# Transformer layer in split float32 on one core: products of the middle pieces alternate between the two token tiles

## The chip, the core and the metric

The kernel runs on one of the eight cores of a Trainium2 chip. The metric is the device time of one execution in microseconds. Three runs of the kernel before took 646.57, 647.06 and 647.47 us; the median is 647.06 us.

## What is computed

One layer of a hybrid network on 256 tokens of width 1024, in float32: a gated feed-forward block, a mixing block whose two arms are a causal depthwise convolution and an attention of 16 heads, and a second feed-forward block. Cut to the matrix products, which are nearly all of the work:

```python
x = x + 0.5 * swiglu(rms_norm(x, ffn1_norm), ffn1_w_gate, ffn1_w_up, ffn1_w_down)   # 1024 -> 2 x 2816 -> 1024
proj = rms_norm(x, mix_norm) @ w_in                                               # 1024 -> 7 x 1024
conv_a, conv_b, q, k, v, gate_a, gate_b = jnp.split(proj, SPLITS, axis=-1)
y_a = silu(layer_norm(causal_depthwise_conv(conv_a * sigmoid(conv_b), ...))) @ w_conv_proj
y_b = attention(q, k, v) @ w_attn_proj                     # 16 heads of 64, causal over 256 tokens
x = x + (sigmoid(gate_a) * y_a + sigmoid(gate_b) * y_b) @ w_out
x = x + 0.5 * swiglu(rms_norm(x, ffn2_norm), ffn2_w_gate, ffn2_w_up, ffn2_w_down)
```

## The kernel before, in words

**Tiles.** The 256 tokens are two token tiles of 128 rows, t = 0 and 1. A chunk is 512 output columns of a weight matrix (`CH`); it needs two accumulators of 128 x 512 float32, one for each token tile, and each fills one PSUM bank. The tag `acc` has three such tiles (line 67), so two chunks in a row share one bank between them. `tr`, three tiles, takes transposes and the attention's small products.

**Split float32.** Every operand is kept as two tiles of type float32r, a rounded `hi` and a rest `lo`; a product is three matmuls, hi by hi, hi by lo and lo by hi. The stationary operand is the transposed activation (`ah(k, t)` and `al(k, t)`, 128 x 128), the moving one is the weight piece (`wh`, `wl`, 128 x 512).

**`gemm` (lines 137 to 178).** A chunk is worked off in pieces of two k-tiles (`KP`): four pieces where the depth is 1024, eleven where it is 2816. For each piece SyncE's queue loads `raw` (line 151), ScalarE rounds it to `hi` (line 100, a cast), and VectorE or GpSimd subtracts to make `lo` (line 102). There are five buffers each of `raw`, `hi` and `lo` (line 37), so the cast of a piece waits until TensorE has read the `hi` of the piece five before it. Then come twelve matmuls (lines 159 to 167): for t, for the two k-tiles, the three products. The first chunk of all runs through `gemm_first` (line 106), which the change leaves alone.

**Other TensorE work.** Between pieces TensorE gets what other parts left in `later` and `bg`: transposes (lines 211, 359, 385, 438, 509, 649) and, in the input projection, the attention, which is a generator advanced by `side`: scores (line 463, four matmuls for a pair of heads, in the upper and the lower 64 rows), `flip` and values (line 524, four matmuls). ScalarE and VectorE do the softmax, the convolution's taps and the norms.

**Who orders it.** The program is recorded in this order, but `schedule_with_timeline_sim=True` (line 824) lets a scheduler of the compiler order each engine's instructions anew by its own estimate of their times; the order on every engine is fixed when the program is built. So a change in `gemm` can move instructions anywhere.

**The seam the prediction speaks of.** `conv_act` (lines 378 to 400) stands between the attention projection and the convolution projection: sixteen transposes of `ynat` into four `tr` tiles (line 385), then on ScalarE a load of the activation table, two Silu activations for each tile (`z`, line 392) and a cast to `u2h` (line 398), then `u2l` on VectorE (line 399). `u2h` and `u2l` are the stationary operands of the next projection.

Of the kernel before, what the change touches and what calls it, by code (L numbers as in the profile page):

```python
# [50 lines left out]
class Build:  # L51
# [85 lines left out]
    def gemm(self, w, c, n, kt, ah, al, pump=0, pool=0.0, split_k=None, side=None):  # L137


        nc = self.nc  # L140
        acc = [self.acc(), self.acc()]
        k0 = 0
        npiece = 0
        sizes = list(split_k) if split_k else []
        while sum(sizes) < kt:
            sizes.append(min(KP, kt - sum(sizes)))
        for kp in sizes:
            raw = self.wp.tile([P, KP * CH], F32, tag="raw", name="raw", bufs=RAW_BUFS)
            hi = self.wp.tile([P, KP * CH], F32R, tag="hi", name="hi", bufs=HI_BUFS)
            lo = self.wp.tile([P, KP * CH], F32R, tag="lo", name="lo", bufs=LO_BUFS)  # L150
            self.last_dma = nc.sync.dma_start(
                raw[:, : kp * n].rearrange("p (k n) -> p k n", n=n), w(c, k0, kp)
            )
            self.share += pool
            pool_lo = self.share >= 1.0
            if pool_lo:
                self.share -= 1.0
            self.split(raw[:, : kp * n], hi[:, : kp * n], lo[:, : kp * n], pool_lo)
            for t in range(2):
                o = acc[t][:, :n]  # L160
                for j in range(kp):
                    k = k0 + j
                    wh, wl = hi[:, j * n : (j + 1) * n], lo[:, j * n : (j + 1) * n]
                    st, sp = k == 0, k == kt - 1
                    nc.tensor.matmul(o, ah(k, t), wh, start=st, stop=False)  # L165
                    nc.tensor.matmul(o, ah(k, t), wl, start=False, stop=False)  # L166
                    nc.tensor.matmul(o, al(k, t), wh, start=False, stop=sp)  # L167
            k0 += kp
            npiece += 1
            if npiece == LATER:  # L170
                self.flush()
            if side is not None:
                self.side += side[1]
                while self.side >= 1:
                    self.side -= 1
                    next(side[0], None)
            self.pump(pump)
        return acc
# [656 lines left out]
```

## Time and profile before

| what | us |
|---|---|
| median of three runs | 647.06 |
| the profiled execution's own time | 646.76 |
| its span, first to last instruction | 644.9 |
| TensorE matmul busy | 638.5 |
| VectorE busy | 371.6 |
| ScalarE busy | 365.9 |
| GpSimd busy | 163.1 |
| DMA, share of 16 engines | 55.5% |

The span is 1.86 us shorter than the execution's own time, which in turn lies 0.30 us under the median. Matmuls overlap in the profile: the duration of one is given as 0.39 us, while the next starts 0.23 us after it, so the busy time of TensorE says only that it is hardly ever empty; its pace is read from the starts.

### The profile page before, as it was taken

What the parts mean: (1) busy time and instruction counts of PE and PEld (TensorE: products, weight loads), DVE (VectorE), ACT (ScalarE), POOL (GpSimd) and SP (SyncE); (2) the same over time, 40 slices, a digit from 0 to 9 for tenths busy, and PEclk for the clock granted to TensorE, in tenths of its full rate; (3) what the DMA queues carried; (4) which work ended last, traced back from release to release, by engine and by line L of the source; (5) the groups of instructions that cost most, each with busy time, mean ns of one, the idle gap of its engine ahead of it and who ended that gap; (6) DMA issues with size and microseconds to landing.
All of it is one profiled execution on the core that took longest, in us unless ns stands there. A gap on an engine that the chain in (4) does not pass through costs nothing.

```text
span 644.9 us, 8142 instructions
## 1 busy us (share of the span) xinstructions
PE 638.5 (99%) x2952; PEld 517.1 (80%) x2952; DVE 371.6 (58%) x625; ACT 365.9 (57%) x549; POOL 163.1 (25%) x83
## 2 busy tenths in 40 slices
PE   9999999999999999999999999999999999999997
PEld 7788888888888888777777778788888888888886
DVE  5655464564552699879314835685664546365541
ACT  6755354443545676977987676944655435444330
POOL 0100000000006999599757564000100000000000
PEclk9999999999999999999999999999999999999999
DMA  8966655567564555544544444364755656556730
GB/s 278 353 228 194 197 170 195 161 194 224 170 200 136 182 167 185 172 131 145 177 153 147 148 146 132 131 223 135 228 161 186 197 175 201 188 167 195 202 124 33
DMA packets 32855, 114.97 MB, mean 178 GB/s; under 512 B 3632, under 2 KB 4912, under 8 KB 32816
## 3 DMA queue, kind: packets, MB, share of 16 engines
q1 hardware_dynamic: 32816, 114.46, 55.5%
q8 instruction: 23, 0.38, 0.2%
q14 instruction: 16, 0.13, 0.1%
HBM read 113.40 MB, written 1.05 MB: 177 GB/s over the span
## 4 chain that ended last, share of the span: by engine, by line
PE 67%; ACT 0%; DVE 0%; issue 0%; DVEq 0%
PE acc L165 20%; PE acc L166 20%; PE acc L167 20%; PE tr L463 2%; PE tr L524 1%; PE tr L211 1%; PE tr L509 1%; PE tr L438 1%; PE tr L359 0%; PE tr L649 0%; ACT z L392 0%; PE tr L385 0%; ACT u2h L398 0%; DVE un L640 0%; DVE ot L748 0%
## 5 line engine op out<-in xcount | busy, mean ns | idle before, releaser
L100 ACT CAST hi<-raw 128x1024 fp32r<-128x1024 f32 (+1 forms) x216 | 223.4, 1037 | 221.2 <-PE acc L167 187.6
L102 DVE TENSOR_TENSOR lo<-raw,hi 128x1024 fp32r<-128x1024 f32 (+1 forms) x156 | 186.6, 1199 | 169.7 <-ACT hi L100 165.3
L102 POOL TENSOR_TENSOR lo<-raw,hi 128x1024 fp32r<-128x1024 f32 x60 | 142.9, 2404 | 213.2 <-ACT hi L100 213.2
L347 DVE SCALAR_TENSOR_TENSOR cv<-uT,cst,cv 128x255 f32<-128x255 f32 (+28 forms) x240 | 95.4, 469 | 10.6 <-ACT cv L343 10.4
L166 PE MATMUL acc<-lo,h1h 128*128 128x512 f32 x224 | 89.0, 397 | 0.0
L165 PE MATMUL acc<-hi,h1h 128*128 128x512 f32 x224 | 88.3, 399 | 0.2 <-DVE un L640 0.2
L167 PE MATMUL acc<-hi,h1l 128*128 128x512 f32 x224 | 87.0, 394 | 0.0
L165 PE MATMUL acc<-hi,h2h 128*128 128x512 f32 x176 | 69.1, 393 | 0.0
L165 PE MATMUL acc<-hi,aTh 128*128 128x512 f32 x176 | 68.8, 391 | 0.0
L167 PE MATMUL acc<-hi,aTl 128*128 128x512 f32 x176 | 68.5, 389 | 0.0
L166 PE MATMUL acc<-lo,aTh 128*128 128x512 f32 x176 | 68.5, 389 | 0.0
L166 PE MATMUL acc<-lo,h2h 128*128 128x512 f32 x176 | 68.5, 390 | 0.0
L167 PE MATMUL acc<-hi,h2l 128*128 128x512 f32 x176 | 67.2, 390 | 0.0
L166 PE MATMUL acc<-lo,hTh 128*128 128x512 f32 x160 | 62.4, 390 | 0.5 <-DVE lo L102 0.5
L165 PE MATMUL acc<-hi,hTh 128*128 128x512 f32 x160 | 62.2, 392 | 0.0
L167 PE MATMUL acc<-hi,hTl 128*128 128x512 f32 x160 | 62.1, 389 | 0.0
L165 PEld LDWEIGHTS acc<-hi,h1h 128*128 128x128 f32 x224 | 42.1, 188 | 11.2 <-issue 2.0
L166 PEld LDWEIGHTS acc<-lo,h1h 128*128 128x128 f32 x224 | 42.1, 188 | 9.4 <-issue 1.7
L167 PEld LDWEIGHTS acc<-hi,h1l 128*128 128x128 f32 x224 | 42.1, 188 | 9.1 <-issue 0.8
L167 PEld LDWEIGHTS acc<-hi,aTl 128*128 128x128 f32 x176 | 33.0, 188 | 6.9
L165 PEld LDWEIGHTS acc<-hi,h2h 128*128 128x128 f32 x176 | 33.0, 188 | 6.8
L165 PEld LDWEIGHTS acc<-hi,aTh 128*128 128x128 f32 x176 | 33.0, 188 | 6.8
(138 smaller groups left out, 788.7 us busy)
## 6 DMA issues: line engine op xcount, KB each, us to landing
raw<-w_in SPq DMA_DIRECT2D x56, 512.0 KB, 4.3
raw<-w2gu SPq DMA_DIRECT2D x44, 512.0 KB, 4.5
raw<-w1gu SPq DMA_DIRECT2D x40, 512.0 KB, 4.7
raw<-w1d SPq DMA_DIRECT2D x22, 512.0 KB, 4.4
raw<-w2d SPq DMA_DIRECT2D x22, 512.0 KB, 4.5
raw<-w_attn SPq DMA_DIRECT2D x8, 512.0 KB, 3.9
raw<-w_conv SPq DMA_DIRECT2D x8, 512.0 KB, 4.0
raw<-w_out SPq DMA_DIRECT2D x8, 512.0 KB, 4.2
```

The costliest lines, as they stand in the source:

```text
L100: nc.scalar.copy(hi, raw)
L102: ins = eng.tensor_tensor(lo, raw, hi.bitcast(F32), ALU.subtract)
L165: nc.tensor.matmul(o, ah(k, t), wh, start=st, stop=False)
L166: nc.tensor.matmul(o, ah(k, t), wl, start=False, stop=False)
L167: nc.tensor.matmul(o, al(k, t), wh, start=False, stop=sp)
L211: nc.tensor.transpose(ps[:, q * S + t * P : q * S + (t + 1) * P], src(t, j + q), self.ident)
L347: nc.vector.scalar_tensor_tensor(o, u, w, o, ALU.mult, ALU.add)
L438: nc.tensor.transpose(ps[:, q * S + t * P : q * S + (t + 1) * P], xs[t][:, (j + q) * P : (j + q + 1) * P], self.ident,)
L463: nc.tensor.matmul(ps[q][:, t * P : t * P + (t + 1) * P], qT[r, b * S + t * P : b * S + (t + 1) * P], kT[r, b * S : b * S + (t + 1) * P], ...
L509: nc.tensor.transpose(ps[:, i * P : (i + 1) * P], pr[:, o : o + P], self.ident)
L524: nc.tensor.matmul(ps[q * HD : (q + 1) * HD, kt * P : S], v[:, kt * D + h * HD : kt * D + (h + 1) * HD], pT[:, o : o + n], start=kt == 0, ...
```

## The change

In every piece but the first and the last of a chunk the loop over the token tiles goes inside: for each k-tile hi by hi goes to t = 0 and then to t = 1, then lo by hi to both, then hi by lo to both. In the first and the last piece the outer loop over t stays. Everywhere the order of the three products of one k-tile becomes hi by hi, activation's lo by weight's hi, activation's hi by weight's lo; before, the weight's lo came second. The number of matmuls, their operands and sizes, the loads and the casts stay as they are.

```diff
-            for t in range(2):
-                o = acc[t][:, :n]
+            ts = ((0,), (1,)) if k0 == 0 or k0 + kp == kt else ((0, 1),)
+            for tt in ts:
                 for j in range(kp):
                     k = k0 + j
                     wh, wl = hi[:, j * n : (j + 1) * n], lo[:, j * n : (j + 1) * n]
                     st, sp = k == 0, k == kt - 1
-                    nc.tensor.matmul(o, ah(k, t), wh, start=st, stop=False)
-                    nc.tensor.matmul(o, ah(k, t), wl, start=False, stop=False)
-                    nc.tensor.matmul(o, al(k, t), wh, start=False, stop=sp)
+                    for a, w_part, i in ((ah, wh, 0), (al, wh, 1), (ah, wl, 2)):
+                        for t in tt:
+                            nc.tensor.matmul(
+                                acc[t][:, :n], a(k, t), w_part, start=st and i == 0,
+                                stop=sp and i == 2,
+                            )
```

In the built programs all three products now stand on line 167, and every later line is numbered three higher (385 becomes 388, 392 becomes 395, 463 becomes 466, 524 becomes 527). `gemm` works off 208 pieces in all; 118 of them are neither first nor last, and in 44 of them all twelve products alternate as built, since the scheduler orders the rest in other ways. Of the neighbouring products of 512 columns with nothing between, 362 pairs changed bank before and 799 do now; 790 pairs had the same stationary tile before and none has now.

**TensorE, second chunk, its first piece (hi_231, lo_232), before.** `acc_228` is t = 0, `acc_229` t = 1; hTh and hTl are the activation's two parts.

```order
L165 MATMUL acc_228<-hi_231,hTh_72 128x512
L165 MATMUL acc_229<-hi_231,hTh_72 128x512
L166 MATMUL acc_228<-lo_232,hTh_72 128x512
L167 MATMUL acc_228<-hi_231,hTl_73 128x512
L165 MATMUL acc_228<-hi_231,hTh_72 128x512
```


The same place now:

```order
L167 MATMUL acc_228<-hi_231,hTh_72 128x512
L167 MATMUL acc_228<-hi_231,hTl_73 128x512
L167 MATMUL acc_229<-hi_231,hTh_72 128x512
L167 MATMUL acc_229<-hi_231,hTl_73 128x512
L167 MATMUL acc_228<-lo_232,hTh_72 128x512
```


Four products that need only `hi` stand ahead of the first that needs `lo`; before there were two.

**TensorE, its second piece (hi_249, lo_250), before.**

```order
L165 MATMUL acc_228<-hi_249,hTh_72 128x512
L165 MATMUL acc_229<-hi_249,hTh_72 128x512
L166 MATMUL acc_228<-lo_250,hTh_72 128x512
L167 MATMUL acc_228<-hi_249,hTl_73 128x512
L165 MATMUL acc_228<-hi_249,hTh_72 128x512
L166 MATMUL acc_228<-lo_250,hTh_72 128x512
L167 MATMUL acc_228<-hi_249,hTl_73 128x512
L166 MATMUL acc_229<-lo_250,hTh_72 128x512
```


The same place now:

```order
L167 MATMUL acc_228<-hi_249,hTh_72 128x512
L167 MATMUL acc_229<-hi_249,hTh_72 128x512
L167 MATMUL acc_228<-hi_249,hTl_73 128x512
L167 MATMUL acc_229<-hi_249,hTl_73 128x512
L167 MATMUL acc_228<-lo_250,hTh_72 128x512
L167 MATMUL acc_229<-lo_250,hTh_72 128x512
L167 MATMUL acc_228<-hi_249,hTh_72 128x512
L167 MATMUL acc_229<-hi_249,hTh_72 128x512
```


Before, four of the twelve steps from the piece's first product to the first of the next piece change the accumulator; now all twelve do.

**TensorE, input projection, values of one pair of heads (`tr_2714`) and the score of another (`tr_2745`, `tr_2746`), before.**

```order
L524 MATMUL tr_2714<-pT_2621,v_1542 64x256 x2
L524 MATMUL tr_2714<-pT_2621,v_1542 64x128 x2
L166 MATMUL acc_2803<-lo_2849,h1h_104 128x512
L167 MATMUL acc_2803<-hi_2848,h1l_105 128x512
L165 MATMUL acc_2803<-hi_2848,h1h_104 128x512
L166 MATMUL acc_2803<-lo_2849,h1h_104 128x512
L167 MATMUL acc_2803<-hi_2848,h1l_105 128x512
L165 MATMUL acc_2802<-hi_2890,h1h_104 128x512
L166 MATMUL acc_2802<-lo_2891,h1h_104 128x512
L167 MATMUL acc_2802<-hi_2890,h1l_105 128x512
L463 MATMUL tr_2745<-kT_1541,qT_1540 128x128
L463 MATMUL tr_2746<-kT_1541,qT_1540 128x128
L463 MATMUL tr_2745<-kT_1541,qT_1540 128x256
L463 MATMUL tr_2746<-kT_1541,qT_1540 128x256
```


The same place now:

```order
L527 MATMUL tr_2714<-pT_2621,v_1542 64x256 x2
L527 MATMUL tr_2714<-pT_2621,v_1542 64x128 x2
L466 MATMUL tr_2745<-kT_1541,qT_1540 128x128
L466 MATMUL tr_2745<-kT_1541,qT_1540 128x256
L167 MATMUL acc_2802<-hi_2848,h1l_105 128x512
L167 MATMUL acc_2803<-hi_2848,h1l_105 128x512
L167 MATMUL acc_2802<-lo_2849,h1h_104 128x512
L167 MATMUL acc_2803<-lo_2849,h1h_104 128x512
L466 MATMUL tr_2746<-kT_1541,qT_1540 128x128
L466 MATMUL tr_2746<-kT_1541,qT_1540 128x256
```


The score was one run of four; now its upper half (`tr_2745`) directly follows the values and its lower half (`tr_2746`) comes four products later.

**TensorE and ScalarE at the seam.** First TensorE before: the last piece of the attention projection is hi_3642, `u2h` belongs to the convolution projection.

```order
L165 MATMUL acc_3586<-hi_3642,oh_1543 128x512
L166 MATMUL acc_3586<-lo_3643,oh_1543 128x512
L167 MATMUL acc_3586<-hi_3642,ol_1544 128x512
L165 MATMUL acc_3586<-hi_3642,oh_1543 128x512
L385 MATMUL tr_3541<-ident_91,ynat_1539 128x128 x3
L385 MATMUL tr_3551<-ident_91,ynat_1539 128x128 x3
L385 MATMUL tr_3561<-ident_91,ynat_1539 128x128 x3
L166 MATMUL acc_3586<-lo_3643,oh_1543 128x512
L167 MATMUL acc_3586<-hi_3642,ol_1544 128x512
L385 MATMUL tr_3571<-ident_91,ynat_1539 128x128 x4
L165 MATMUL acc_3663<-hi_3666,u2h_3459 128x512
```


Now:

```order
L167 MATMUL acc_3586<-hi_3642,oh_1543 128x512
L167 MATMUL acc_3586<-hi_3642,ol_1544 128x512
L167 MATMUL acc_3586<-lo_3643,oh_1543 128x512
L388 MATMUL tr_3541<-ident_91,ynat_1539 128x128 x3
L388 MATMUL tr_3551<-ident_91,ynat_1539 128x128 x3
L388 MATMUL tr_3561<-ident_91,ynat_1539 128x128 x3
L388 MATMUL tr_3571<-ident_91,ynat_1539 128x128 x4
L167 MATMUL acc_3663<-hi_3666,u2h_3459 128x512
```


ScalarE before (line 100 casts a piece, line 392 is Silu with its table load, line 398 makes `u2h`):

```order
L100 CAST hi_3702<-raw_3701 128x1024
L100 CAST hi_3720<-raw_3719 128x1024
L392 ACT_TABLE_LOAD
L392 ACTIVATE z_3546<-tr_3541,cst_70 128x256 x2
L392 ACTIVATE z_3556<-tr_3551,cst_70 128x256 x2
L398 CAST u2h_3459<-z_3546 128x512
L100 CAST hi_3744<-raw_3743 128x1024
L398 CAST u2h_3459<-z_3556 128x512
```


Now:

```order
L100 CAST hi_3702<-raw_3701 128x1024
L100 CAST hi_3720<-raw_3719 128x1024
L100 CAST hi_3744<-raw_3743 128x1024
L395 ACT_TABLE_LOAD
L395 ACTIVATE z_3546<-tr_3541,cst_70 128x256 x2
L395 ACTIVATE z_3556<-tr_3551,cst_70 128x256 x2
L401 CAST u2h_3459<-z_3546 128x512
L401 CAST u2h_3459<-z_3556 128x512
```


On TensorE the two products between the transposes of the last run went ahead of them, and the run is now thirteen transposes with nothing between. On ScalarE the cast of hi_3744 moved from behind the first `u2h` to ahead of the table load. hi_3744 is the fifth cast after hi_3642 and takes its buffer.

The start of a chunk in the input projection (before: line 165 into `acc_1657`, then line 165 into `acc_1658`, which waits) differs in one row: now a second product into `acc_1657`, activation's lo by the same hi, stands between the two.

## Rows read from the trace of the kernel before

**Rows 1.** The page: span, busy time of the engines, TensorE's clock in 40 slices.

```profile
span 644.9 us, 8142 instructions
...
PE 638.5 (99%) x2952; PEld 517.1 (80%) x2952; DVE 371.6 (58%) x625; ACT 365.9 (57%) x549; POOL 163.1 (25%) x83
...
PEclk9999999999999999999999999999999999999999
```

**Rows 2.** TensorE waits from 30 us on: engine, line, releaser: total us, times, longest.

```profile
PE acc L165 <- ACT u2h L398: 0.8, 1, 0.8
PE acc L165 <- DVE un L640: 0.2, 1, 0.2
```

**Rows 3.** Timeline of TensorE, one bank (start us, duration us, engine, line, operation, count).

```profile
28.23 0.39 PE L165 MATMUL acc<-hi,hTh 128*128 128x512 f32 x1
...
30.95 0.39 PE L165 MATMUL acc<-hi,hTh 128*128 128x512 f32 x1
```

**Rows 4.** Timeline of TensorE, second piece of the second chunk, four bank changes.

```profile
20.07 0.62 PE L165 MATMUL acc<-hi,hTh 128*128 128x512 f32 x2
20.52 0.39 PE L166 MATMUL acc<-lo,hTh 128*128 128x512 f32 x1
...
22.79 0.39 PE L165 MATMUL acc<-hi,hTh 128*128 128x512 f32 x1
```

**Rows 5.** Timeline, second chunk begins (TensorE; bracket: idle before and releaser).

```profile
16.58 0.63 PE L165 MATMUL acc<-hi,hTh 128*128 128x512 f32 x2
...
17.69 0.51 PE L166 MATMUL acc<-lo,hTh 128*128 128x512 f32 x1 [0.47 <-DVE lo L102]
```

**Rows 6.** Timeline of TensorE at the start of a chunk of the input projection.

```profile
207.75 0.39 PE L165 MATMUL acc<-hi,h1h 128*128 128x512 f32 x1
...
208.30 0.50 PE L165 MATMUL acc<-hi,h1h 128*128 128x512 f32 x1 [0.16 <-DVE un L640]
```

**Rows 7.** Timeline of TensorE: split scores, then whole values and a whole score, each with what follows.

```profile
276.47 0.86 PE L524 MATMUL tr<-pT,v 128*64 128x256 f32 x6
277.26 0.92 PE L463 MATMUL tr<-kT,qT 64*128 64x128 f32 x4
278.11 0.50 PE L166 MATMUL acc<-lo,h1h 128*128 128x512 f32 x1
...
279.69 0.92 PE L463 MATMUL tr<-kT,qT 64*128 64x128 f32 x4
280.54 0.50 PE L166 MATMUL acc<-lo,h1h 128*128 128x512 f32 x1
...
314.74 0.87 PE L524 MATMUL tr<-pT,v 128*64 128x256 f32 x8
315.54 0.50 PE L166 MATMUL acc<-lo,h1h 128*128 128x512 f32 x1
...
317.61 0.93 PE L463 MATMUL tr<-kT,qT 64*128 64x128 f32 x8
318.46 0.50 PE L165 MATMUL acc<-hi,h1h 128*128 128x512 f32 x1
```

**Rows 8.** Timeline of TensorE and ScalarE between the attention and the convolution projection.

```profile
402.88 0.39 PE L167 MATMUL acc<-hi,ol 128*128 128x512 f32 x1
...
403.35 1.06 ACT L100 CAST hi<-raw 128x1024 fp32r<-128x1024 f32 x1 [0.31 <-PE acc L167]
...
404.42 1.28 ACT L392 ACT_TABLE_LOAD   x1
...
405.53 1.15 PE L385 MATMUL tr<-ident,ynat 128*128 128x128 f32 x9
...
406.06 1.94 ACT L392 ACTIVATE z<-tr,cst 128x256 f32<-128x256 f32 x4 [0.35 <-PE tr L385]
...
407.87 0.63 ACT L398 CAST u2h<-z 128x512 fp32r<-128x512 f32 x1
...
408.55 0.50 PE L165 MATMUL acc<-hi,u2h 128*128 128x512 f32 x1 [0.77 <-ACT u2h L398]
```

## The prediction

> **What bounds the kernel now.** I read the page first. TensorE is busy 638.5 of the 644.9 us, VectorE and ScalarE under 60% of it, and TensorE's clock stands at full in every slice [rows 1]. Next the waits: from 30 us on TensorE waited just twice for another engine, 0.8 us for ScalarE's `u2h` and 0.2 us for VectorE's `un` [rows 2]. So the time is the number of matmuls times their step, plus a few holes, and whatever lengthens TensorE's own sequence lengthens the kernel. Last I read the step. In a stretch in which one bank takes everything, 28.23 to 30.95 us, twelve products take 2.72 us, 0.2267 us each [rows 3]. A difference of 0.2% of the time, 1.3 us, is about what a measurement of this kernel can tell from no change; a hole of that size at TensorE decides which side the result falls on.
>
> **The alternation itself: 0.** The piece at 20.07 us also has twelve steps, and four of them change the bank, two of those one right after the other (the row of two products at 20.07 and the next at 20.52). It takes 20.07 to 22.79, again 2.72 us [rows 4]. The pair of steps with two bank changes takes 0.45 us, like any two. So a product pays 0.2267 us whether its predecessor wrote its bank or the other one, and 437 more bank changes (799 less 362) are worth nothing. Nor does the loss of the 790 pairs with one stationary tile cost anything: there were as many weight loads as matmuls, 2952 of each [rows 1], and in the stretch of one bank, where a third of the steps keep the stationary tile, the pace is that of the others.
>
> At full clock 512 columns would take 0.2133 us (2.4 GHz), so 13 ns of each step have no name. The Trainium skill (TensorE: Matmul & The Clock Gate, Back-to-back issue gap) gives about 216 ns for 512 columns in isolation, which no row here shows; if its difference of 11 ns to our step were a price of staying in one bank, 437 changes would bring, as an estimate from that page, 4.8 us, and the time would be 644.7. The sum stays with the rows, and the rival below goes by the 13 ns.
>
> What is left is what the scheduler did with the new program. Four places differ in a way that TensorE feels.
>
> **Second chunk, first piece: -0.45 us.** TensorE starts two products at 16.58, and the third, which needs `lo`, starts at 17.69 where 17.03 was due, released by VectorE [rows 5]. Hence 0.66 us are lost. Now four products stand ahead of the first `lo`, two more, which fill 2 x 0.2267 = 0.45 us; 0.2 us stay lost. Nothing takes it back later, as TensorE does not wait again until 207 us [rows 2]. Bounds: 0 and -0.66.
>
> **Start of a chunk of the input projection: -0.23 us.** The product at 208.30 was due 0.2267 after 207.75 and came 0.55 after it, 0.32 us late, behind VectorE's read of the accumulator [rows 6]. One product now stands ahead of it that did not: -0.23. Bounds: 0 and -0.32.
>
> **One score split in two: +0.85 us.** The attention's score of four small matmuls takes from 317.61 until the next product at 318.46, 0.85 us; four values from 314.74 to 315.54, 0.80. Half a score takes just as long as a whole one: 277.26 to 278.11 directly behind values, and 279.69 to 280.54 alone, 0.85 each [rows 7] (the profile records each of these matmuls twice, so a whole score reads x8 and a half x4). I take it that in a whole score the matmuls of the upper and of the lower rows run side by side, and that a half has no partner. One score that was whole is now split, its first half behind the values of another pair of heads, its second alone. The products are interrupted twice there before and after, so the price is one further half, 0.85 us. The other splits are in both programs. Bounds: 0, if the half behind the values hides, and 1.7, if neither half finds its price in the old one.
>
> **The seam: +2.28 us.** This is the largest term. Call T the start of the last run of transposes, 405.53. Before, ScalarE cast hi_3720 from 403.35, loaded the table from 404.42 to 405.70, waited 0.35 us for the first transposes and began `z` at 406.06; `u2h` came at 407.87, and the first product of the convolution projection at 408.55, so T + 3.02 [rows 8]. TensorE filled that with 13 transposes and two products.
>
> In the new order the cast of hi_3744 stands ahead of the table load. It takes the buffer of hi_3642, the last piece of the attention projection, and that piece's products are now all ahead of T. The last that reads hi_3642 is the last but one product, begun 0.45 us before T and ended 0.39 us later. A cast starts 0.08 us after such an end: 402.88 + 0.39 = 403.27, the cast at 403.35 [rows 8]. So hi_3744 starts at T + 0.02, the table load 1.06 later at T + 1.08, `z` 1.28 later at T + 2.36, where transposes are long done, and the first product of the next projection 408.55 - 406.06 = 2.49 us after `z`, at T + 4.85. T itself lies 0.45 us later, since the two products that stood between the transposes are ahead of it. Counted from the old T the product comes at 5.30 instead of 3.02: +2.28 us. What is late next: the fourth `tr` tile reuses the first one's buffer and must wait for its `z`, so of TensorE's hole about 2.3 us lie in front of the last four transposes (half of the 1.94 us of `z` ends at T + 3.33, nine transposes at about T + 1) and about 1 us in front of the product.
>
> What is queued behind the cast on ScalarE is the table load, all `z` and `u2h`; SyncE's loads and VectorE's `lo` run ahead by several pieces and nobody on TensorE misses them there. The second pair of `u2h` casts now stands behind a second table load and the gate's sigmoids; I add nothing for it and leave it to the bound. Bounds: 1.22, if the cast of 1.06 us escaped to before T, and 3.34, if a further one fell into the chain.
>
> **Sum.** -0.45 - 0.23 + 0.85 + 2.28 = +2.45 us. The profiled execution took 646.76 us by its own time (1.86 us more than its span), which makes 649.21; the median of the runs lies 0.30 higher, and I predict 647.06 + 2.45 = **649.5 us**, 0.38% slower.
>
> **Rivals.** (a) *Faster, because a bank change is cheaper after all.* The point that decides is the step in an alternating piece: below 0.2211 us (2.45 / 437 = 5.6 ns less) the change wins. With all 13 ns gone from 437 steps it would give 5.8 us back: 647.06 + 2.45 - 5.8 = 643.7. Against it stand the equal 2.72 us of both stretches, with two changes in a row among them [rows 3, 4]; for it, only that before no stretch alternates throughout. 7%.
>
> (b) *The same, because the seam hides.* If the cast of hi_3744 is done before T, the seam costs 1.22; with half of the price of the split score and both gains at their bounds the time is 647.06 + 1.22 + 0.43 - 0.66 - 0.32 = 647.7. Against it: the order on ScalarE is fixed, and the buffer it waits for is plain from the order. 13%.
>
> (c) *Slower by more.* The attention's softmax chain on ScalarE and VectorE has moved with everything else, and no wait there was visible before [rows 2]; one tile that comes late because a table load of 1.28 us [rows 8] stands ahead of it costs TensorE that much: 650.8. 14%.
>
> (d) *The clock falls.* The clock stands at full with 362 bank changes already [rows 1]. If it fell to 1.2 GHz in the 44 alternating pieces, their 528 products of 0.2267 us would take 120 us more, 769 us. The Trainium skill (TensorE: Matmul & The Clock Gate, A second HAM failure mode: psum-queue depth-cycling) tells of a kernel that cycled through banks and whose clock went up and down; the trace has no sign of that here. 1%.
>
> My forecast, about 648.5 to 650.3, has 65%.
>
> **Chances and range.** Slower by over 0.2% is the forecast, (c) and (d): 0.80. Within 0.2%: 0.13. Faster: 0.07. The range of eight in ten leaves out (a), (d), half of (b) and the tail of (c): 647.8 to 650.8.
>
> **What will show it.** In alternating pieces a step of 0.2267 us; on TensorE's list of waits transposes (line 388) for `z` with about 2.3 us and the product of `u2h` with about 1 us; at 17 us a hole of 0.2 instead of 0.66; in the attention one more half score of 0.85 us. Wrong would be: a shorter step, a table load at the seam that starts within 0.1 us of T or before, or new waits between 210 and 400 us.

## The result: slower by more than forecast

The changed kernel takes 651.36 us (four runs, 650.56 to 651.91) against 646.82 us for the kernel before on the same chip (four runs, 646.44 to 647.47). The ratio is 1.0068, 95% interval 1.0051 to 1.0086. The forecast was 649.5 with a range to 650.8: the sign is right, the size is 4.5 us instead of 2.45, and the range misses it by 0.6. One further execution of the kernel before, on the chip of *after_again*, took 914.32 us at a mean granted clock of 0.753 and is left out of all comparisons.

The page of the changed kernel, to be laid beside [rows 1] (PE is TensorE and PEld its weight loads, DVE is VectorE, ACT ScalarE, POOL GpSimd):

```profile
span 649.3 us, 8155 instructions
...
PE 640.7 (99%) x2952; PEld 518.4 (80%) x2952; DVE 373.1 (57%) x625; ACT 366.7 (56%) x549; POOL 163.4 (25%) x83
...
PEclk9999999999999999999999999899999999999999
```

The same number of matmuls is busy 2.2 us longer, of which the forecast had only the split score's 0.85. One of the 40 slices of TensorE's clock shows an 8, which the forecast did not have at all. The list of TensorE's waits from 30 us on, which answers to [rows 2], has the two waits of the forecast (about 2.3 and about 1 us):

```profile
PE tr L388 <- ACT z L395: 2.3, 1, 2.3
PE acc L167 <- ACT u2h L401: 0.8, 1, 0.8
```

The timeline of an alternating piece, the second of the second chunk, which answers to [rows 4] (start us, duration us, engine, line, operation, count):

```profile
20.41 0.62 PE L167 MATMUL acc<-hi,hTh 128*128 128x512 f32 x2
...
23.13 0.62 PE L167 MATMUL acc<-hi,hTh 128*128 128x512 f32 x2
```

Twelve products with a bank change at every step take 23.13 - 20.41 = 2.72 us, to the hundredth what four changes took before. The split score, beside [rows 7]:

```profile
315.09 0.87 PE L527 MATMUL tr<-pT,v 128*64 128x256 f32 x8
315.89 0.92 PE L466 MATMUL tr<-kT,qT 64*128 64x128 f32 x4
316.74 0.73 PE L167 MATMUL acc<-hi,h1l 128*128 128x512 f32 x2
...
317.87 0.92 PE L466 MATMUL tr<-kT,qT 64*128 64x128 f32 x4
318.72 0.50 PE L167 MATMUL acc<-hi,h1h 128*128 128x512 f32 x1
```

Each half takes 0.85 us, the first directly behind the whole values (315.09 to 315.89, 0.80). The seam, TensorE and ScalarE, beside [rows 8]:

```profile
407.02 1.14 PE L388 MATMUL tr<-ident,ynat 128*128 128x128 f32 x9
407.04 1.06 ACT L100 CAST hi<-raw 128x1024 fp32r<-128x1024 f32 x1 [0.30 <-PE acc L167]
...
408.11 1.28 ACT L395 ACT_TABLE_LOAD   x1
...
409.40 1.93 ACT L395 ACTIVATE z<-tr,cst 128x256 f32<-128x256 f32 x4
...
410.48 0.66 PE L388 MATMUL tr<-ident,ynat 128*128 128x128 f32 x4 [2.31 <-ACT z L395]
...
411.21 1.14 ACT L401 CAST u2h<-z 128x512 fp32r<-128x512 f32 x2
...
411.89 1.65 PE L167 MATMUL acc<-hi,u2h 128*128 128x512 f32 x3 [0.76 <-ACT u2h L401]
...
413.34 0.63 PE L167 MATMUL acc<-hi,u2l 128*128 128x512 f32 x1
413.76 0.63 PE L167 MATMUL acc<-lo,u2h 128*128 128x512 f32 x1
414.19 0.63 PE L167 MATMUL acc<-hi,u2h 128*128 128x512 f32 x1
```

With T = 407.02, the start of the last run of transposes, the cast stands at T + 0.02, the table load at T + 1.09, `z` at T + 2.38 and the first product at T + 4.87; the forecast had 0.02, 1.08, 2.36 and 4.85. What it did not have is in the last three rows: the products that follow start 0.42 and 0.43 us apart. The stretches of that time, one row each (columns: stretch, its length, busy us and count of TensorE's matmuls, its weight loads, VectorE, ScalarE and GpSimd, then TensorE's granted clock, the DMA share, GB/s):

```profile
403.00:411.38 8.38, 5.83 (x32) 4.53 (x30) 6.23 (x7) 7.38 (x11) 1.49 (x1) 1.00 0.64 212
411.38:414.79 3.41, 2.90 (x7) 2.32 (x8) 1.29 (x2) 3.09 (x7) 0.00 (x0) 0.50 0.69 239
414.79:418.00 3.21, 3.21 (x16) 2.63 (x15) 0.00 (x0) 3.20 (x5) 0.00 (x0) 1.00 0.00 0
```

Right behind the hole the granted clock is 0.50, which is 1.2 GHz, for 3.41 us; then it is full again. From 411.89 to 414.79 seven products start where 2.90 / 0.2267 = 12.8 would have.

**The ledger of the two profiled executions**, made from the start of the n-th product of 512 columns in each, the kernel now less the kernel before:

| place | forecast | profiled |
|---|---|---|
| start of the second chunk | -0.45 | +0.34 |
| start of the input projection | -0.23 | -0.21 |
| split score | +0.85 | +0.89 |
| seam, idle time | +2.28 | +2.28 (from +1.06 to +3.34) |
| seam, clock | none | +1.32 (to +4.66) |
| output projection | none | -0.28 |
| span | +2.45 | +4.4 |

Two rows are wrong, then: the start, and the clock that nobody priced; the -0.28 at the output projection stays unexplained. What had to be shown is that the hole takes the clock down, not the alternation, and that the alternation costs nothing itself.

### The profile page after: what moved, and what is told of

Same layout as the page of the kernel before. It is cut to its first block, busy times and chain, and to the rows that moved or that the text cites. A ratio compares the mean times of both kernels' runs of the same rounds, so it can differ in the third digit from the quotient of the medians.

```text
span 649.3 us, 8155 instructions
## 1 busy us (share of the span) xinstructions
PE 640.7 (99%) x2952; PEld 518.4 (80%) x2952; DVE 373.1 (57%) x625; ACT 366.7 (56%) x549; POOL 163.4 (25%) x83
## 4 chain that ended last, share of the span: by engine, by line
PE 96%; DMA 2%; ACT 1%; DVE 0%; SPq 0%; issue 0%; DVEq 0%; ACTq 0%
PE acc L167 88%; PE tr L214 2%; PE tr L466 2%; PE tr L527 1%; DMA raw<-w1gu 1%; PE tr L512 1%; DMA raw<-w1f 1%; PE tr L441 1%; ACT hi L100 0%; DVE lo L102 0%; ACT z L395 0%; PE tr L652 0%; PE tr L362 0%; ACT L395 0%; SPq L121 0%
## 5 line engine op out<-in xcount | busy, mean ns | idle before, releaser
L350 DVE SCALAR_TENSOR_TENSOR cv<-uT,cst,cv 128x255 f32<-128x255 f32 (+29 forms) x240 | 95.4, 468 | 3.5 <-ACT cv L346 3.2
L167 PE MATMUL acc<-hi,h1h 128*128 128x512 f32 x224 | 86.0, 399 | 0.0
L167 PE MATMUL acc<-lo,h1h 128*128 128x512 f32 x224 | 84.7, 396 | 0.0
L167 PE MATMUL acc<-hi,h2h 128*128 128x512 f32 x176 | 66.5, 393 | 0.0
L167 PE MATMUL acc<-lo,h2h 128*128 128x512 f32 x176 | 66.4, 390 | 0.0
L167 PE MATMUL acc<-hi,aTh 128*128 128x512 f32 x176 | 60.0, 391 | 0.0
L167 PE MATMUL acc<-lo,aTh 128*128 128x512 f32 x176 | 59.8, 389 | 0.0
L167 PE MATMUL acc<-hi,aTl 128*128 128x512 f32 x176 | 59.7, 389 | 0.0
L167 PEld LDWEIGHTS acc<-lo,aTh 128*128 128x128 f32 x176 | 33.0, 188 | 6.9
L167 PEld LDWEIGHTS acc<-lo,h2h 128*128 128x128 f32 x176 | 33.0, 188 | 6.9
```

The source lines that it names most:

```text
L167: nc.tensor.matmul(acc[t][:, :n], a(k, t), w_part, start=st and i == 0, stop=sp and i == 2,)
L350: nc.vector.scalar_tensor_tensor(o, u, w, o, ALU.mult, ALU.add)
```

## Experiments

Each was timed in five rounds beside the kernel before on the same chip; a ratio is read as a difference where its 95% interval excludes 1. The mean granted clock of every execution is given where it decides. In the executions of the kernel before that the comparisons use it is 0.998 to 1.0.

**The two halves of the change, each alone.** *alternate_only* keeps the old order of the three products, *order_only* the old loop over the token tiles.

```diff
-                    for a, w_part, i in ((ah, wh, 0), (al, wh, 1), (ah, wl, 2)):
+                    for a, w_part, i in ((ah, wh, 0), (ah, wl, 1), (al, wh, 2)):
```

> Half of the change: the token tile is the inner loop in the middle pieces, but the three products keep the old order (hi by hi, hi by lo, lo by hi). As built, every engine has the instructions of the kernel before in the same order, only the products of 512 columns go to the banks in another order: 794 neighbouring pairs change the bank instead of 362. Theory (a bank change costs nothing; the 4.5 us come from the order at the seam, the hole there that takes the clock down, and one split score): 646.8 us, ratio 0.999 to 1.001, clock full at the seam, step 0.227 us. Rival (each of the 437 more changes costs some 10 ns, or they take the clock down): 432 x 10.4 ns = 4.5 us more, 651.3 us, ratio 1.007.

```diff
-            ts = ((0,), (1,)) if k0 == 0 or k0 + kp == kt else ((0, 1),)
+            ts = ((0,), (1,))
```

> The other half: the new order of the three products (hi by hi, lo by hi, hi by lo) with the token tile outside everywhere; 372 bank changes as built, against 362 before. Theory (what the new order of the products lets the scheduler do is the whole loss): here it builds a seam with holes of about 0.2 us before the last transposes and 2.0 and 0.7 us before the first products of the next projection (0.2 and 1.0 before), and two scores whose halves stand one behind the other instead of side by side, 0.85 us more each; +3.1 us from these, 649.9 us, and 651.2 if the clock falls behind the hole. Rival (the banks make the loss): 646.8 us.

*alternate_only*: 646.87 us against 646.87, ratio 1.0001 (0.9993 to 1.0010). The interval reaches 0.65 us above 1, so each of the 432 further bank changes costs under 1.5 ns. Its clock is 0.999 or 1.0 in all eleven executions, and its waits are those of [rows 2]:

```profile
PE acc L167 <- ACT u2h L401: 0.8, 1, 0.8
PE acc L167 <- DVE un L643: 0.2, 1, 0.2
```

Within that interval the alternation is free, and it does not take the clock down.

*order_only*: 648.04 us, ratio 1.0017 (1.0008 to 1.0026), less than the 649.9 that I expected with a full clock. Two terms of that were too large. The two scores whose halves stand one behind the other take 0.86 us each in its profile, like whole ones, so in them the order of the four small matmuls made no difference. And the waits before the first products of the next projection are 1.71 and 0.38 us, not 2.0 and 0.7. Its clock is 0.996 or 0.997 in four of eleven executions (650.06, 648.87, 648.48 and 649.84 us), and 0.999 or 1.0 in the other seven (647.45 to 648.41). The two waits in the profiled execution, one of the four:

```profile
409.75 0.96 PE L167 MATMUL acc<-hi,u2h 128*128 128x512 f32 x3 [1.71 <-ACT u2h L401]
411.10 0.50 PE L167 MATMUL acc<-hi,u2l 128*128 128x512 f32 x1 [0.38 <-DVE u2l L402]
```

There the clock is full until 411.73 us, 1.98 us after the first product, and 0.50 for 3.41 us from then on: the fall need not come at the end of the wait.

The halves do not add up to the whole: 0 and 1.2 us alone, 4.5 together. What differs is what the scheduler makes of each program.

**The seam covered.** On TensorE the last piece of the attention projection is ordered behind the first twelve transposes of `ynat`, in the changed kernel (*after_covered*) and in the kernel before (*before_covered*). `tr3` is the last of these transposes.

```diff
+            hold = self.tr3 if cover and k0 + kp == kt else None
...
-            for tt in ts:
+            with self.tc.issue_after(hold.ins) if hold is not None else nullcontext():
+                for tt in ts:
```

> The changed kernel with its 800 bank changes, and one order more: on TensorE the last piece of the attention projection comes behind the first twelve transposes of ynat, so that its twelve products fill the time of ScalarE's table load, z and u2h. Theory: the holes of 2.3 and 0.8 us at the seam shrink to one of about 0.6 before the first transpose and 0.2 before a product, the clock stays full, 651.4 - 2.1 - 1.3 = 648.0 us, ratio 1.002. Rival (the alternation takes the clock down, the hole only happens to lie there): the clock falls all the same and the time is 649.3 us; rival (banks cost 10 ns each): about 651.

> The kernel before with the same order at the seam, to see what the seam is worth without any alternation. Theory: the holes of 0.2 and 1.0 us become 0.5 us before the first product and 0.4 us before the second half of u2h: 646.4 us, ratio 0.999. Rival (the seam's holes are not on the path that sets the end): 646.8 us. If the cover hid everything: 645.7 us.

*after_covered*: 647.53 us, ratio 1.0009 (1.0000 to 1.0018), clock 0.999 or 1.0 in all eleven executions. With 800 bank changes kept, the loss is 0.7 us instead of 4.5, and the interval touches 1. From 30 us on TensorE waits once:

```profile
PE tr L390 <- DVE ynat L380: 0.3, 1, 0.3
```

*before_covered*: 646.56 us, ratio 0.9995 (0.9987 to 1.0004), so not told apart from the kernel before. With the seam covered in both, the two differ by about 1.0 us, of which the split score explains 0.85.

**Is it the hole that takes the clock down?** Three runs. *after_again* is the changed kernel unchanged. *after_filled* is the changed kernel with ten extra products, which nobody reads, in the hole. *before_late_z* is the kernel before with three extra Silu activations ahead of `z`, which make a hole in it.

```diff
+            if c == 6:
+                fill = self.cv()
+                with self.tc.issue_after(tr.ins):
+                    for _ in range(10):
+                        tr = nc.tensor.matmul(
+                            fill, self.fill[:, :P], self.fill[:, :CH], start=True, stop=True
+                        )
```

```diff
+                if c == 0:
+                    for _ in range(3):
+                        j = self.tmp.tile([P, CH], F32, tag="sg", name="sj", bufs=3)
+                        after = nc.scalar.activation(j, ps, AF.Silu)
```

> The changed kernel once more, on the chip of the three runs beside it, for its clock in each execution. Theory: ratio 1.006 to 1.008, the mean clock 0.996 to 0.997 in every execution, since the hole at the seam is there in every one. Rival (the fall of the clock is chance): some executions at 0.999 or 1.0, about 1.3 us shorter.

> The changed kernel with ten extra products of 512 columns between the twelfth and the thirteenth transpose of ynat, into a PSUM tile that nobody reads (they are work added, the result stays the same). They take 10 x 0.227 = 2.27 us in the hole of 2.3 us, so the order and the times of ScalarE stay. Theory (the long idle stretch takes the clock down, and that costs 1.3 us): the clock stays full, 651.4 - 1.3 = 650.1 us, ratio 1.005. Rival (the clock falls for another reason, the alternation or a time in the run): it falls all the same, 651.4 us or more, ratio 1.007.

> The kernel before with three extra Silu activations of 128x512 on ScalarE ahead of z, into a tile that nobody reads (work added, result the same); no alternation, old order of the products. They delay z by some 3 x 0.75 us, which makes a hole at the seam as long as that of the changed kernel. Theory: holes of about 2.4 us before the last transposes and 1 us before the first product of the next projection, the clock falls behind them: 646.9 + 2.3 + 1.3 = 650.5 us, ratio 1.0055, mean clock 0.996 to 0.997. Rival (a hole alone does not take the clock down, it needs the alternation): clock full, 649.2 us, ratio 1.0035.

*after_again*: 652.12 us, ratio 1.0083 (1.0070 to 1.0097). The clock fell in every execution, as in the first four: two have a mean clock of 0.996 (651.61 and 651.63 us), two of 0.994 (652.61 and 653.40). The profiled one is of the latter, and in it the clock is at 1.2 GHz for 6.83 us (410.92 to 417.75) instead of 3.41. So this run missed my expectation of 0.996 to 0.997 throughout, to the side of a longer fall.

*after_filled*: 649.92 us, ratio 1.0046 (1.0033 to 1.0058), clock 0.998 to 1.0. Order and times at the seam are those of the changed kernel, only the hole is full:

```profile
406.62 1.14 PE L396 MATMUL tr<-ident,ynat 128*128 128x128 f32 x9
407.52 2.53 PE L390 MATMUL cv<-oh 128*128 128x512 f32 x10
410.08 0.66 PE L396 MATMUL tr<-ident,ynat 128*128 128x128 f32 x4
411.49 0.97 PE L167 MATMUL acc<-hi,u2h 128*128 128x512 f32 x3 [0.76 <-ACT u2h L409]
412.30 0.42 PE L167 MATMUL acc<-hi,u2l 128*128 128x512 f32 x1
412.56 0.39 PE L167 MATMUL acc<-lo,u2h 128*128 128x512 f32 x1
412.79 0.40 PE L167 MATMUL acc<-hi,u2h 128*128 128x512 f32 x1
```

The first product comes 4.87 us after the start of the last run of transposes, as without the filling, but the ones behind it soon run 0.23 us apart (412.56 to 412.79). The last piece of the chain of work up to 416 us, in *after_again* and then in *after_filled* (start us, duration us, what, count), has the price:

```profile
411.54 4.64 PE acc L167 x10
411.49 4.67 PE acc L167 x19
```

In the same time ten products get done in the one and nineteen in the other. Ten products of useless work make the kernel faster, by 0.0083 - 0.0046 = 0.37% of 647 us, 2.4 us, beside *after_again* on the same chip, and the two intervals do not meet. Since order and times at the seam are the same otherwise, that is the clock's share. It mixes two kinds of fall: the two executions with a mean clock of 0.996 lie 1.7 us above 649.92, the two with 0.994 2.7 and 3.5. *after_filled* itself is slower than the kernel before by 3.0 us (2.1 to 3.8 by the interval), which holds the 2.45 that I had predicted without the clock.

*before_late_z*: 651.89 us, ratio 1.0072 (1.0060 to 1.0085), clock 0.994 to 0.997 in all five executions. There is no alternation in it and no new order of products, and yet the clock falls:

```profile
409.42 0.66 PE L385 MATMUL tr<-ident,ynat 128*128 128x128 f32 x4 [1.45 <-ACT z L397]
411.78 0.80 PE L165 MATMUL acc<-hi,u2h 128*128 128x512 f32 x1 [1.71 <-ACT u2h L403]
...
412.80 0.63 PE L165 MATMUL acc<-hi,u2h 128*128 128x512 f32 x1
413.23 0.63 PE L166 MATMUL acc<-lo,u2h 128*128 128x512 f32 x1
```

I had expected the hole in another split (2.4 and 1 us; it came as 1.45 and 1.71) and 650.5 us, with a mean clock of 0.996 to 0.997. The two executions at 0.997 took 651.17 and 650.46 us; in the other three the mean is 0.994, and they took 651.89 to 652.47. The rival, that the clock needs the alternation, falls.

**A version that beats both.** The parts that proved good were put together: *order_covered* is the new order without alternation with the covered seam; *order_covered_whole* also chains the four value matmuls of a pair of heads on TensorE so that none is split, and *after_covered_whole* is that with the alternation.

```diff
+            mm = None
             for kt in range(2):
-                for q in range(2):
+                for q in (1, 0):
...
+                    with self.tc.issue_after(mm.ins) if mm is not None else nullcontext():
+                        mm = nc.tensor.matmul(
```

> The new order of the three products without alternation, and the last piece of the attention projection behind the first twelve transposes. Theory: of the order alone's 648.0 us the holes of the seam go, 2.1 us in the profiled execution, against some 0.6 us of new ones, and the clock no longer falls in any execution: 646.3 us, ratio 0.999, mean clock 0.999 or 1.0 throughout. Rival (the order of products costs elsewhere too): 647.5 us or more.

> The new order of the products without alternation, the seam covered as in the run before, and the four small matmuls of a pair's values chained on TensorE with the upper head first, so that the scheduler no longer splits them: as built all eight values stand whole; before it split six. Theory (a split value costs 0.78 and 0.80 us in place of 1.0, so half a microsecond each; the price of the attention lies in what is split): 6 x 0.55 = 3.3 us less in the attention, of which new waits of about 2.8 us for a gate's product and ynat on VectorE take most: 645.0 to 645.6 us, ratio 0.9965 to 0.998. Rival (the splits hide beside other work): 646.2 us or more, since the waits come on top.

> The same with the alternation of the changed kernel (784 bank changes as built). Theory (banks cost nothing): as its neighbour without alternation within 0.3 us, 645.0 to 645.6 us. Rival (banks cost 10 ns each): 4 us more than its neighbour.

*order_covered*: 646.15 us, ratio 0.9992 (0.9983 to 1.0001), clock 0.999 or 1.0: as expected, but not told apart from no change. *order_covered_whole*: 646.87 us, ratio 0.9987 (0.9977 to 0.9998); *after_covered_whole*: 646.70, ratio 0.9987 (0.9979 to 0.9996). Both miss what I expected by over 1 us. The attention did get shorter: the last product ahead of the seam's transposes starts at 397.80 us in *order_covered_whole* and at 402.30 in *order_covered*, 4.5 us apart, of which 0.6 were there from the start of the second chunk on. But the seam came so early that `ynat` was not ready:

```profile
397.80 0.39 PE L169 MATMUL acc<-lo,oh 128*128 128x512 f32 x1
400.28 0.76 PE L390 MATMUL tr<-ident,ynat 128*128 128x128 f32 x3 [2.09 <-DVE ynat L380]
402.24 2.04 PE L390 MATMUL tr<-ident,ynat 128*128 128x128 f32 x9 [1.20 <-DVE ynat L380]
403.93 0.77 PE L169 MATMUL acc<-hi,oh 128*128 128x512 f32 x1
404.50 0.63 PE L169 MATMUL acc<-hi,ol 128*128 128x512 f32 x1
404.93 0.63 PE L169 MATMUL acc<-lo,oh 128*128 128x512 f32 x1
```

The forecast of these runs had new waits of about 2.8 us, and the profile shows 4.7 (3.3 and 0.7 for `ynat`, 0.7 for the gate); the clock it again did not have. Of the twelve executions of *order_covered_whole* two kept it full and took 644.13 and 644.41 us, less than I had expected; the five at 0.997 took 645.85 to 646.88, the five at 0.993 or 0.994 took 646.93 to 647.74. In *after_covered_whole* two of eleven kept it full, with 644.82 and 644.68 us. It is the omission of the first forecast again: new waits counted, their clock not. The last two runs fill that hole with fourteen products that nobody reads.

```diff
+            if hold is not None:
+                fill = self.cv()
+                with self.tc.issue_after(self.prev.ins):
+                    for _ in range(14):
+                        nc.tensor.matmul(fill, ah(0, 0), self.fill[:, :CH], start=True, stop=True)
```

> The run with covered seam and whole values, new order of the products, no alternation, and fourteen extra products of 512 columns (work added, nobody reads them) on TensorE ahead of the first transposes of ynat, where that run stood idle for 2.1 us and again for 1.2. They take 3.2 us and end before the later of the two waits does. Theory (idle TensorE takes the clock down): the clock stays full in every execution, and the time is that of the few executions of that run whose clock stayed full, 644.1 to 644.4 us: ratio 0.9955 to 0.996. Rival (the clock does not depend on the hole): mean clock 0.993 to 0.997 again and 646.9 us; rival (the extra products lie on the path): 647.5 us or more.

> The same with the alternation of the changed kernel (some 780 bank changes). Theory (neither banks nor alternation cost or bring anything): as its neighbour within 0.3 us, 644.3 to 644.8 us, ratio 0.996, clock full. Rival (banks cost 10 ns each): 4 us more than its neighbour; rival (alternation takes the clock down): mean clock 0.997 or less, 646.7 us.

*order_whole_filled*: 645.35 us, ratio 0.9972 (0.9961 to 0.9983). *after_whole_filled*, with the alternation: 644.84 us, ratio 0.9969 (0.9957 to 0.9981). The clock is 0.999 or 1.0 in all thirteen executions, where it had fallen in 19 of 23 without the filling. Both are faster than the kernel before by 0.3%; the changed kernel was slower by 0.7%. The first misses its expected 644.1 to 644.4 us by 1.0, and no run shows what that is made of; the second lies at the upper end of its 644.3 to 644.8. And as these runs lay on another chip, their gain of 0.15 and 0.18% over the unfilled ones is no clear difference: the intervals overlap. The place in *after_whole_filled*:

```profile
398.66 3.34 PE L164 MATMUL cv<-oh 128*128 128x512 f32 x14
401.84 0.49 PE L395 MATMUL tr<-ident,ynat 128*128 128x128 f32 x3
402.83 1.20 PE L395 MATMUL tr<-ident,ynat 128*128 128x128 f32 x9 [0.51 <-DVE ynat L385]
403.79 0.48 PE L174 MATMUL acc<-hi,oh 128*128 128x512 f32 x1
404.10 0.40 PE L174 MATMUL acc<-hi,ol 128*128 128x512 f32 x1
404.34 0.40 PE L174 MATMUL acc<-lo,oh 128*128 128x512 f32 x1
```

The wait behind the filling is 0.51 us. Behind the first step the products run 0.24 us apart (404.10 to 404.34), where in *order_covered_whole* they ran 0.43 apart (404.50 to 404.93). With and without alternation the times differ by less than their intervals, once more.

## Why the prediction was right in its parts and wrong in its size

**The alternation itself: 0.** Right, shown twice: 2.72 us for a piece with twelve changes, and *alternate_only* at 1.0001. Rival (a), that a bank change is cheaper, falls: a step is 0.227 us with and without one. The Trainium skill (TensorE: Matmul & The Clock Gate, Back-to-back issue gap) gives about 216 ns for 512 columns in isolation; the difference to the trace is no price of staying in one bank.

**Second chunk, first piece: -0.45.** The term is right, and the ledger hides it. Four products now precede the first `lo`, as forecast. The wait ahead of that `lo` is 18.46 - 18.01 - 0.23 = 0.22 us in the changed kernel, the 0.2 of the forecast; it is 0.64 to 0.70 us in the four profiles with the old order of products and 0 to 0.23 in the ten with the new one. What the forecast did not have is that the first pieces of the second chunk land at another time in each execution. In the profiled one ScalarE waited longer for its load; its cast before, and then the changed kernel's cast and products:

```profile
15.32 1.05 ACT L100 CAST hi<-raw 128x1024 fp32r<-128x1024 f32 x1 [1.39 <-DMA raw<-w1gu]
...
16.10 1.05 ACT L100 CAST hi<-raw 128x1024 fp32r<-128x1024 f32 x1 [3.02 <-DMA raw<-w1gu]
...
17.20 0.50 PE L167 MATMUL acc<-hi,hTh 128*128 128x512 f32 x1 [0.48 <-ACT hi L100]
...
18.01 0.40 PE L167 MATMUL acc<-hi,hTl 128*128 128x512 f32 x1
18.46 0.50 PE L167 MATMUL acc<-lo,hTh 128*128 128x512 f32 x1
```

So the chunk began at 17.20 us and not at 16.58, and the ledger has +0.34. The 61st product of 512 columns starts at 20.07, 20.45, 20.53 and 20.89 us in the four profiles with the old order of products, and between 19.36 and 20.73, 20.07 on average, in the ten with the new one. The averages lie 20.49 - 20.07 = 0.42 us apart, which is no more than the spread within either group. The profiled execution of the kernel before had the earliest start of the four.

**Start of a chunk of the input projection: -0.23.** Right: -0.21.

**One score split in two: +0.85.** Right: +0.89. *after_covered* less *before_covered* leaves 1.0 us, which it would explain for the most part. The reason behind the term, that the two halves of a whole score run side by side, is shown by no run.

**The seam: +2.28.** Its idle time is right to 0.02 us at each of its steps, and the two waits came as 2.31 and 0.76 us for 2.3 and about 1. The term is wrong in what it counts: I priced the time in which TensorE stands still and let the products behind it run at 0.2267 us. That is the step that failed. Between the last product of the attention projection, which starts at 406.79 us, and 411.89 there are thirteen transposes, two waits and no product. The clock drops to 1.2 GHz, and each product costs 0.43 us until it is back: +1.32 us in the profiled execution, some 2.4 by *after_filled* beside *after_again*. Where the clock is kept up the kernel takes 649.92 us, near the forecast of 649.5.

**Rival (d), the clock falls,** was given 1% and tied to the alternation. The event came by another cause, at a hole that I had worked out to 0.02 us. The Trainium skill (TensorE: Matmul & The Clock Gate, A second HAM failure mode: psum-queue depth-cycling) tells of a kernel that cycles through PSUM banks, with short idle times of TensorE between its groups of matmuls, and whose clock goes up and down. Of that, bank changes alone do nothing here: with 794 of them in *alternate_only* and 800 in *after_covered* the clock is 0.999 or 1.0 in all 22 executions. The section before it in the Trainium skill (TensorE: Matmul & The Clock Gate, HAM oscillation — how this bites in real kernels) tells of a kernel in which TensorE waits for a DMA ahead of each group of products and the group then starts at the low clock. The trace agrees with that for a wait on ScalarE, with a granted clock of 0.50 from 411.38 to 414.79 after the wait of 2.31 us and within that of 0.76; *after_filled* and *before_late_z* show it from both sides.

Rivals (b) and (c) do not apply: the seam did not hide, and no new wait stood in the attention.

Left open: why the clock falls in only four of eleven executions of *order_only*, in ten of twelve of *order_covered_whole* and in nine of eleven of *after_covered_whole*, with one order of instructions each. No run separates the executions of one program. Nor was the cast of `hi_3744` moved by itself; that it stands first in the chain is read from the rows, and the covered seam took the whole hole away, not that cast alone.

## What to carry to other kernels

Price a hole on TensorE twice: the time it stands still, and the slow products behind it, here 1.3 to 2.4 us on top of 2.3; a forecast that finds a new hole should ask for the clock at once. Where real work cannot be moved into a hole, products that nobody reads may pay for themselves, as in *after_filled* beside *after_again*, if they end before the wait does. And where a compiler's scheduler orders the engines, test the parts of an edit alone: the part it was named for did nothing here, and all of its cost came from what the scheduler made of the rest.

## What the runs showed of the hardware

- A product of 512 columns costs 0.227 us whether it goes to the bank of its predecessor or to the other one (the kernel before and the changed kernel); by *alternate_only* the two differ by under 1.5 ns.
- At a granted clock of 0.50 the same product starts 0.43 us after its predecessor (the changed kernel, *after_again*, *before_late_z*).
- Half a score takes as long as a whole one, 0.85 us (the kernel before and the changed kernel); a whole score takes 0.86 also where the two matmuls of one half stand ahead of the two of the other (*order_only*).
- With waits of TensorE of 2.31 and 0.76 us at the seam the clock fell in 8 of 8 executions (the changed kernel, *after_again*), with 1.45 and 1.71 in 5 of 5 (*before_late_z*), with 2.09 and 1.20 in 10 of 12 (*order_covered_whole*), with 1.71 and 0.38 in 4 of 11 (*order_only*). With a single one of 0.8 it fell in no compared execution (the kernel before, *alternate_only*, *after_filled*).
- One program falls to the lower clock in some of its executions and not in others, and for 3.41 us in one profiled execution of the changed kernel and 6.83 in another; the times then stand in groups (644.13 and 644.41, then five with a median of 646.38, then five with one of 647.02 us in *order_covered_whole*).
